# RWKV in a two-layer hybrid backbone: both directions' inverses on the diagonal of one 128x128 square

## The chip, the core and the metric

The kernel runs on one core of a Trainium2 chip. The metric is the device time of one execution in microseconds (us); the kernel before took 3027.57 us, the median of three runs (3020.59 to 3033.45). Engines: TensorE (PE; PEld is its weight load), VectorE (DVE), ScalarE (ACT), GpSimd (POOL), and SyncE (SP), which issues the transfers.

## What is computed

Two layers of a backbone over 256 latent and 256 context tokens of 1024 features. A layer is a half-step SwiGLU, a token mixing of three branches (retention, windowed attention, RWKV-7) with gates and an output projection, and a second half-step SwiGLU. The change touches RWKV-7 alone: 8 heads of 64, a forward and a backward scan, first over the context, then over the latent tokens from the context's final state.

```python
def rwkv7_scan(r, w, k, a, v, kk, s0, reverse):
    def step(S, inp):
        r_t, w_t, k_t, a_t, v_t, kk_t = inp
        sa = -jnp.einsum('bhvk,bhk->bhv', S, kk_t)
        S = (S * w_t[:, :, None, :] + sa[..., None] * (kk_t * a_t)[:, :, None, :]
             + v_t[..., None] * k_t[:, :, None, :])
        return S, jnp.einsum('bhvk,bhk->bhv', S, r_t)
    ...
    ys_f, S_f = rwkv7_scan(r_s, *dirs_s[0], v_s, kk_s, zero_rw, False)
    ys_b, S_b = rwkv7_scan(r_s, *dirs_s[1], v_s, kk_s, zero_rw, True)
    yx_f, _ = rwkv7_scan(r_x, *dirs_x[0], v_x, kk_x, S_f, False)
    yx_b, _ = rwkv7_scan(r_x, *dirs_x[1], v_x, kk_x, S_b, True)
    rwkv_x = rwkv_output(yx_f + yx_b, r_x, v_x, dirs_x, g_x, p)
```

## The kernel before

The big weight products (`mm3`, L186 to L188) run in three passes of a split format (fp32r, a high and a low part); one such pass is one TensorE instruction. All other products are f32, and each is two instructions in the trace. Weights come by DMA as `raw`, ScalarE makes `whi` (L114), VectorE `wlo` (L115).

RWKV works on chunks of 64 tokens: 4 chunks a stream, 2 streams (0 context, 1 latent), 4 pairs of heads, 2 layers. That is 16 rounds; the context of layer 1 needs no outputs, so 12 of the 16 make outputs (`want_y`). A round has five parts:
- `rw_prep` makes decays, and for each direction the operands `ar` (alpha, rho) and `kb` (kappa, beta). L945 transposes `kb` to `kbT`. L961 makes the Gram products; VectorE masks them into `gk` (L966) and, for outputs, into `tg` rows 64 to 127 (L968). ScalarE cuts the 32x32 diagonal blocks out (L964), and GpSimd inverts them (L989, L990).
- `rw_merge` fetches the inverted blocks as `z`. ScalarE (L1007) and VectorE (L1008) put them on the diagonal of `tg` rows 0 to 63, products of 32x32 (L1016, L1021) make the blocks off the diagonal. There is one `tg` tile for each stream and direction: 64 rows for the inverse, 64 for the triangular part of the outputs.
- `rw_vals` centres the values, one product for each chunk on 64 of the rows (L1033), and ScalarE copies them into `ve` for each direction (L1035, L1036) and into a block-diagonal tile `vb` (L1039).
- `rw_chain` goes through the chunks, j = 0 to 3, forward from the first and backward from the last, one direction after the other, each in one PSUM tile of the two under `rx`. For one direction: L1058 and L1060 add up values and state; L1062 (ScalarE) negates; L1065 is the inverse times that, two products for the two heads on a 64x64 tile; L1067 (ScalarE) copies the result into `ve`; L1069 makes the state's update, L1081 (VectorE) blends it into the state; L1086 multiplies the triangular part, again two 64x64 products; L1088 to L1092 (VectorE) add up the outputs `ya` on rows 64 to 127.
- `rw_out` normalises the outputs and multiplies gate and bonus.

The order of the work in token mixing is written as a list of names (`ORDER`: A and C are `rw_prep` of the two streams, B and D the rest, with retention, attention and gates between). Within that, a scheduler at build time puts the instructions of each engine in a row by its own estimates; the engines then run their rows in order.

```python
for j in range(4):
    for d in range(2):
        q = j if d == 0 else 3 - j
        x = ps("rx")
        PE.matmul(x[0:n, 0:128], gk[d][:, q, 0:n], vb[:, q], ...)
```

## Time and profile before

| | |
|---|---|
| median of 3 runs | 3027.57 us |
| span of the profiled execution | 3030.5 us |
| TensorE busy | 2924.9 us, 97% |
| VectorE busy | 2042.5 us, 67% |
| ScalarE busy | 1322.2 us, 44% |
| GpSimd busy | 382.4 us, 13% |
| mean granted TensorE clock | 0.967 |

The profile is of one execution. Busy times of TensorE count an instruction from its start to its modelled end, and neighbours overlap. The clock is given in parts of 2.4 GHz; a granted 0.50 is 1.2 GHz. The token mixing of layer 0 lies between some 400 and 1350 us, that of layer 1 between 2100 and 2830 us.

### The profile page before, as it was taken

What the parts mean: (1) busy time and instruction counts of PE and PEld (TensorE: products, weight loads), DVE (VectorE), ACT (ScalarE), POOL (GpSimd) and SP (SyncE); (2) the same over time, 40 slices, a digit from 0 to 9 for tenths busy, and PEclk for the clock granted to TensorE, in tenths of its full rate; (3) what the DMA queues carried; (4) which work ended last, traced back from release to release, by engine and by line L of the source; (5) the groups of instructions that cost most, each with busy time, mean ns of one, the idle gap of its engine ahead of it and who ended that gap; (6) DMA issues with size and microseconds to landing.
All of it is one profiled execution on the core that took longest, in us unless ns stands there. A gap on an engine that the chain in (4) does not pass through costs nothing.

```text
span 3030.5 us, 49119 instructions
## 1 busy us (share of the span) xinstructions
PE 2924.9 (97%) x17249; PEld 2436.6 (80%) x17249; DVE 2042.5 (67%) x4625; ACT 1322.2 (44%) x2832; POOL 382.4 (13%) x1076
## 2 busy tenths in 40 slices
PE   8999998999989999999999999999999999989999
PEld 7888887777777777888888888888778788778999
DVE  7977678774684565666756566566777676657755
ACT  3222246554454544343223332233656465555554
POOL 0000003332032121000000000000043433230000
PEclk9999999897989999999999999999979898999999
DMA  7655445341343144544535344444544244156554
GB/s 271 232 182 190 151 127 159 103 127 31 110 131 92 50 138 141 178 136 160 190 134 169 95 157 161 132 135 139 164 123 128 74 143 120 38 175 191 175 185 157
DMA packets 276439, 431.48 MB, mean 142 GB/s; under 512 B 80608, under 2 KB 98144, under 8 KB 276192
## 3 DMA queue, kind: packets, MB, share of 16 engines
q1 hardware_dynamic: 276192, 428.35, 44.8%
q8 instruction: 135, 2.21, 0.3%
q14 instruction: 112, 0.92, 0.1%
HBM read 398.74 MB, written 25.82 MB: 140 GB/s over the span
## 4 chain that ended last, share of the span: by engine, by line
PE 84%; POOL 5%; DVE 4%; DMA 3%; issue 2%; ACT 1%; SPq 1%; POOLq 0%; DVEq 0%; ACTq 0%
PE ps_mm L187 21%; PE ps_mm L186 21%; PE ps_mm L188 21%; POOL cst L990 2%; POOL cst L989 2%; PE ps_rf L961 2%; PE ps_mm L364 1%; PE ps_sc L532 1%; PE ps_po L542 1%; PE ps_po L762 1%; PE ps_rx L1065 1%; PE ps_rx L1058 1%; PE ps_rx L1069 1%; DVE wlo L115 1%; PE ps_rx L1086 1%
## 5 line engine op out<-in xcount | busy, mean ns | idle before, releaser
L114 ACT CAST whi<-raw 128x512 fp32r<-128x512 f32 x1070 | 648.6, 618 | 921.6 <-PE ps_mm L187 729.5
L115 DVE TENSOR_TENSOR wlo<-raw,whi 128x512 fp32r<-128x512 f32 x1070 | 728.9, 691 | 379.1 <-PE ps_mm L188 231.6
L186 PE MATMUL ps_mm<-hall,whi 128*128 128x512 f32 (+1 forms) x2320 | 846.6, 365 | 5.3 <-DVE cst L203 3.3
L188 PE MATMUL ps_mm<-hall,wlo 128*128 128x512 f32 (+1 forms) x2320 | 845.4, 365 | 2.1 <-DVE wlo L115 2.1
L187 PE MATMUL ps_mm<-hall,whi 128*128 128x512 f32 (+1 forms) x2320 | 840.1, 362 | 0.4 <-DVE hall L214 0.4
L186 PEld LDWEIGHTS ps_mm<-hall,whi 128*128 128x128 f32 x2320 | 444.1, 192 | 81.5 <-issue 8.3
L188 PEld LDWEIGHTS ps_mm<-hall,wlo 128*128 128x128 f32 x2320 | 443.0, 191 | 78.4 <-issue 3.9
L187 PEld LDWEIGHTS ps_mm<-hall,whi 128*128 128x128 f32 x2320 | 443.7, 191 | 72.8 <-issue 0.9
L186 PE MATMUL ps_mm<-hid,whi 128*128 128x512 f32 (+1 forms) x737 | 260.6, 354 | 0.0
L187 PE MATMUL ps_mm<-hid,whi 128*128 128x512 f32 (+1 forms) x737 | 260.0, 354 | 0.0
L188 PE MATMUL ps_mm<-hid,wlo 128*128 128x512 f32 (+1 forms) x737 | 257.5, 354 | 0.0
L989 POOL TENSOR_TENSOR cst<-acc,cst 128x60 f32<-128x60 f32 (+24 forms) x496 | 172.6, 348 | 490.2 <-DMA acc<-ad__11118 54.1
L841 POOL TENSOR_TENSOR ll<-lora,lh 64x256 fp32r<-64x256 f32 x16 | 11.9, 744 | 1475.1 <-ACT lh L838 1062.7
L990 POOL TENSOR_TENSOR cst<-cst 128x60 f32<-128x60 f32 (+24 forms) x496 | 178.6, 360 | 38.3
L236 DVE SCALAR_TENSOR_TENSOR ft<-m,cd 128x1024 bf16<-128x1024 f32 x136 | 162.7, 1218 | 6.5 <-DMA m<-ada 6.5
L237 DVE SCALAR_TENSOR_TENSOR m<-m,cd 128x1024 f32<-128x1024 f32 x136 | 165.0, 1218 | 0.7
L186 PEld LDWEIGHTS ps_mm<-hid,whi 128*128 128x128 f32 x737 | 139.2, 189 | 19.5
L187 PEld LDWEIGHTS ps_mm<-hid,whi 128*128 128x128 f32 x737 | 139.1, 189 | 19.3
L188 PEld LDWEIGHTS ps_mm<-hid,wlo 128*128 128x128 f32 x737 | 138.5, 189 | 19.5
L187 PE MATMUL ps_mm<-wlo,hall 128*128 128x256 f32 x416 | 132.7, 319 | 15.2 <-DVE wlo L115 14.9
L373 DVE SCALAR_TENSOR_TENSOR x<-ps_mm,cst,x 128x256 f32<-128x256 f32 x136 | 60.9, 480 | 103.6 <-PE ps_mm L188 101.3
L186 PE MATMUL ps_mm<-whi,hall 128*128 128x256 f32 x416 | 121.7, 294 | 0.2
(326 smaller groups left out, 4369.2 us busy)
## 6 DMA issues: line engine op xcount, KB each, us to landing
m<-ada SPq DMA_DIRECT2D x136, 512.0 KB, 4.3
raw<-w1b SPq DMA_DIRECT2D x271, 256.0 KB, 3.2
raw<-w0b SPq DMA_DIRECT2D x270, 256.0 KB, 2.9
raw<-w0a SPq DMA_DIRECT2D x132, 256.0 KB, 2.9
raw<-w0c SPq DMA_DIRECT2D x132, 256.0 KB, 3.0
raw<-w1a SPq DMA_DIRECT2D x132, 256.0 KB, 2.9
raw<-w1c SPq DMA_DIRECT2D x132, 256.0 KB, 3.0
gd<-ft SPq DMA_DIRECT2D x24, 256.0 KB, 2.6
```

Of the source, the lines that this page charges most:

```text
L114: nc.scalar.copy(hi, raw)
L115: nc.vector.tensor_sub(lo, raw, hi.bitcast(F32))
L186: PE.matmul(o, w[0], h[0], start=start, stop=False)
L187: PE.matmul(o, w[0], h[1], start=False, stop=False)
L188: PE.matmul(o, w[1], h[0], start=False, stop=stop)
L236: V.scalar_tensor_tensor(junk, raw, 1.0, st["cond"][0], ALU.mult, ALU.mult, accum_out=md[:, kt, 0:1])
L237: V.scalar_tensor_tensor(raw, raw, 1.0, st["cond"][1], ALU.mult, ALU.mult, accum_out=md[:, kt, 1:2])
L364: PE.matmul(o[:, p], w[k, j][q], hl(H[k], p)[0], start=(k == 0 and q == 0 and p.start == c.start), stop=False)
L373: V.scalar_tensor_tensor(xs[n][:, CS[s]], o[:, CS[s]], gate[:, n, s:s + 1], xs[n][:, CS[s]], ALU.mult, ALU.add)
L961: PE.matmul(ov[:, q, 0:n], kb[d][hs, q].rearrange("p a t -> p (a t)"), ar[d][hs, q].rearrange("p a t -> p (a t)")[:, 0:n], start=True, sto ...
L989: G.tensor_tensor(w, acc[j // 16][:, j % 16, j + 1:32].unsqueeze(1).to_broadcast([128, m, n]), tt[:, 0:m, j:j + 1].to_broadcast([128, m, n ...
L990: G.tensor_tensor(tt[:, 0:m, j + 1:32], tt[:, 0:m, j + 1:32], w, ALU.add)
```

## The change

The two directions share tiles. `tg` is gone; for each stream there are `tt` and `tr`, each 128x128 for a head and a step: the forward inverse on the rows and columns 0 to 63, the backward one on 64 to 127, in `tr` the triangular parts likewise; the two other quarters hold zeros, set once a layer by GpSimd (L1156) in place of small loads of zeros. The backward direction's chunks lie in reversed order, so that step j of both directions is one slot. To fit, the backward direction keeps alpha and rho, kappa and beta, and its values on the other half of the rows.

`rw_chain` takes both directions in one step: two PSUM tiles, `xa` and `xb`; the values and states of both directions, both negations, then one product a head for both inverses (L1076, a 128x128 tile, 64 columns), two copies, both state updates, and one product a head for both triangular parts (L1101). The outputs gather on both halves of the rows: two ScalarE copies and two VectorE sums a step, and `rw_out` adds the halves. `rw_vals` centres two chunks by one product (L1043), with copies of half the size. In `rw_merge` the copies of the inverse follow the products, and the backward blocks go through a tile of their own.

```diff
     def rw_merge(X, st):
-        z, tn, xm = mk([64, 2, 8, 32], "z", 2), mk([32, 16, 32], "rb", 3)[:, 0:8], mk([64, 16, 32], "rb", 3)[:, 0:8]
+        z, tb, xm = mk([64, 2, 8, 32], "z", 2), mk([64, 16, 32], "rb", 3), mk([64, 16, 32], "rb", 3)[:, 0:8]
+        tn, zt = tb[0:32, 0:8], tb[:, 8:16]
...
-        tg = X["tg"]
-        tu = [tg[d].rearrange("p h c t -> p (h c) t") for d in range(2)]
+        hc = lambda t: t.rearrange("p (h c) t -> p h c t", h=2)
+        fw, bw = X["tt"][0:64, :, :, 0:64], X["tt"][64:128, :, ::-1, 64:128]
         V.transpose(fl(tn), fl(z[0:32, 0]))
         for b in range(2):
             bs = slice(32 * b, 32 * b + 32)
-            A.copy(tu[0][bs, :, bs], z[bs, 0])
-            V.transpose(tu[1][bs, :, bs], z[bs, 1])
+            V.transpose(fl(zt[bs]), fl(z[bs, 1]))
...
+        for b in range(2):
+            bs = slice(32 * b, 32 * b + 32)
+            A.copy(fw[bs, :, :, bs], hc(z[bs, 0]))
+            A.copy(bw[bs, :, :, bs], hc(zt[bs]))
...
     def rw_vals(s, R, st, want_y, X):
-        for q in range(4):
-            PE.matmul(o[0:64, q * 128:q * 128 + 128], v[:, c.start + q * 64:c.start + q * 64 + 64], st["cm"], start=True, stop=True)
-        ov = o.rearrange("p (c d) -> p c d", c=4)
-        A.copy(ve[0][0:64], ov[0:64])
-        A.copy(ve[1][0:64], ov[0:64])
-        for h in range(2):
-            hs = slice(64 * h, 64 * h + 64)
-            A.copy(vb[hs, :, hs], ov[0:64, :, hs])
+        for i in range(2):
+            PE.matmul(o[:, i * 128:i * 128 + 128], v[:, c.start + i * 128:c.start + i * 128 + 128], st["cm"], start=True, stop=True)
+        ov = o[:, 0:256].rearrange("p (c d) -> p c d", c=2)
+        for i in range(2):
+            A.copy(ve[0][64:128, i::2], ov[HV[i]])
+            A.copy(ve[1][0:64, i::2], ov[HV[i]])
+            for h in range(2):
+                A.copy(vb[HV[h], i::2, HV[h]], ov[HV[i], :, HV[h]])
...
     def rw_chain(l, p, s, R, st, want_y, want_u, X):
         for j in range(4):
+            qs = (j, 3 - j)
+            xa, xb = ps("rx"), ps("rx")
+            for d, q in enumerate(qs):
+                U = R["U"][d]
+                rows = slice(0, 128) if want_y else HV[d]
+                xd = xa[rows, d * 128:d * 128 + 128]
+                PE.matmul(xd, gk[d][:, q, rows], vb[:, q], start=True, stop=(U is None))
+                if U is not None:
+                    PE.matmul(xd, ar[d][:, q].rearrange("p a t -> p (a t)")[:, rows], U, start=False, stop=True)
+            rr = sm(128, "rr", 2)
             for d in range(2):
-                A.activation(rr, x[0:64, 0:128], AF.Copy, scale=-1.0)
-                for h in range(2):
-                    hs = slice(64 * h, 64 * h + 64)
-                    PE.matmul(x[64:128, 128 + 64 * h:192 + 64 * h], tg[d][0:64, h, q], rr[:, hs],
-                              start=True, stop=True)
-                A.copy(ve[d][64:128, q], x[64:128, 128:256])
+                A.activation(rr[HV[d]], xa[HV[d], d * 128:d * 128 + 128], AF.Copy, scale=-1.0)
+            for h in range(2):
+                PE.matmul(xa[:, 256 + 64 * h:320 + 64 * h], tt[:, h, j], rr[:, HV[h]], start=True, stop=True)
+            for d, q in enumerate(qs):
+                A.copy(ve[d][HV[d], q], xa[HV[d], 256:384])
...
-                if want_y:
-                    for h in range(2):
-                        hs = slice(64 * h, 64 * h + 64)
-                        PE.matmul(x[64:128, 384 + 64 * h:448 + 64 * h], tg[d][64:128, h, q], ve[d][64:128, q, hs], start=True, stop=True)
-                    if q in seen:
-                        V.tensor_tensor(ya[64:128, q], ya[64:128, q], x[64:128, 0:128], ALU.add)
-                        V.tensor_tensor(ya[64:128, q], ya[64:128, q], x[64:128, 384:512], ALU.add)
-                    else:
-                        V.tensor_copy(ya[64:128, q], x[64:128, 0:128])
-                        V.tensor_tensor(ya[64:128, q], ya[64:128, q], x[64:128, 384:512], ALU.add)
-                        seen.add(q)
+            if want_y:
+                uu = sm(128, "uu", 2)
+                V.tensor_copy(uu, xa[:, 256:384])
+                for d, q in enumerate(qs):
+                    A.copy(ya[HV[1 - d], q], xa[HV[1 - d], d * 128:d * 128 + 128])
+                for h in range(2):
+                    PE.matmul(xb[:, 256 + 64 * h:320 + 64 * h], tr[:, h, j], uu[:, HV[h]], start=True, stop=True)
+                for d, q in enumerate(qs):
+                    V.tensor_tensor(ya[HV[1 - d], q], ya[HV[1 - d], q], xb[HV[1 - d], 256:384], ALU.add)
...
     def mix_consts(l, mark):
-        st["tg"] = {(s, d): mk([128, 2, 4, 64], "tg", 4) for s in range(2) for d in range(2)}
+        st["tt"], st["tr"] = ([mk([128, 2, 4, 128], n, 2) for _ in range(2)] for n in ("tt", "tr"))
+        for t in (*st["tt"], *st["tr"]):
+            G.memset(t, 0.0)
```

Three places show how the rows of instructions change. A row with xN holds N products in a run; names behind a line are output, inputs and the size of the output.

TensorE in layer 0, heads' pair 0, latent tokens, third step of the chain; L762, L759, L742, L743 and L746 are attention's products. Before:

```order
L762 MATMUL ps_po<-aT,kv 64x128 x4
L759 MATMUL ps_ap<-cst,ae 128x128 x3
L1065 MATMUL ps_rx<-cst,tg 64x64 x2
L759 MATMUL ps_ap<-cst,ae 128x128
L742 MATMUL ps_sc<-kd,qT 128x512
L743 MATMUL ps_sc<-kl,qT 128x512
L746 MATMUL ps_sc<-pa,cst 128x128
L188 MATMUL ps_mm<-hall,wlo 128x512
L1065 MATMUL ps_rx<-cst,tg 64x64 x2
L186 MATMUL ps_mm<-hall,whi 128x512
```

And now:

```order
L187 MATMUL ps_mm<-hall,whi 128x512
L188 MATMUL ps_mm<-hall,wlo 128x512
L762 MATMUL ps_po<-aT,kv 64x128 x4
L1076 MATMUL ps_rx<-cst,tt 128x64 x2
L186 MATMUL ps_mm<-hall,whi 128x512
```

Where two groups of two 64x64 products stood apart, one for each direction, one group of two stands for both.

TensorE in layer 0, pair 0, context tokens: the end of `rw_merge` and the centred values. Before:

```order
L542 MATMUL ps_po<-ft 128x128 x2
L1016 MATMUL ps_rx<-rb,cst 32x32 x8
L1016 MATMUL ps_rx<-z,cst 32x32 x8
L1033 MATMUL ps_rx<-cst,rr_v 64x128 x4
L542 MATMUL ps_po<-ft 128x128 x2
```

And now:

```order
L542 MATMUL ps_po<-ft 128x128 x2
L1022 MATMUL ps_rx<-rb,cst 32x32 x8
L1022 MATMUL ps_rx<-z,cst 32x32 x8
L1043 MATMUL ps_rx<-cst,rr_v 128x128 x2
L542 MATMUL ps_po<-ft 128x128 x2
```

Four products on half of the columns of the array become two on all of them, in the same place.

ScalarE in the same chain as the first place; L548, L560 and L572 belong to retention and gates. Before:

```order
L1062 ACTIVATE cst<-ps_rx 64x128
L1067 COPY ve<-ps_rx 64x128
L1062 ACTIVATE cst<-ps_rx 64x128
L548 ACTIVATE ft,cst<-ps_po 128x128 x2
L1074 ACTIVATE cst<-cst 128x128
```

And now:

```order
L1074 ACTIVATE cst<-ps_rx 64x128 x2
L548 ACTIVATE ft,cst<-ps_po 128x128 x4
L560 ACTIVATE ft<-ps_mm 128x512
L572 ACTIVATE ft<-ps_mm 128x512
L1078 COPY ve<-ps_rx 64x128 x2
L1099 COPY rb<-ps_rx 64x128 x2
```

The negations (L1062, now L1074) and the value copies (L1067, now L1078) of the two directions stand in pairs, and the output copies (L1099) follow.

## Rows read from the trace of the kernel before

**Rows 1.** The page: span, busy time by engine, the chain by engine.

```profile
span 3030.5 us, 49119 instructions
PE 2924.9 (97%) x17249; PEld 2436.6 (80%) x17249; DVE 2042.5 (67%) x4625; ACT 1322.2 (44%) x2832; POOL 382.4 (13%) x1076
PE 84%; POOL 5%; DVE 4%; DMA 3%; issue 2%; ACT 1%; SPq 1%; POOLq 0%; DVEq 0%; ACTq 0%
```

**Rows 2.** Span of the core and its mean granted clock.

```profile
core 0: 3030.5 us, clock 0.967
```

**Rows 3.** One window: PE, PEld, DVE, ACT, POOL busy; clock, DMA share, GB/s.

```profile
696.00:727.00 31.00, 30.90 (x160) 22.20 (x161) 11.46 (x32) 10.62 (x31) 7.79 (x28) 0.50 0.11 29
```

**Rows 4.** TensorE groups by shape: busy us, mean ns, idle before.

```profile
L1065 PE MATMUL ps_rx<-cst,tg 64*64 64x64 f32 x512 | 55.1, 234 | 1.9 <-ACT cst L1062 1.8
...
L1086 PE MATMUL ps_rx<-ve,tg 64*64 64x64 f32 x384 | 39.9, 232 | 4.7 <-DVE cst L1081 3.7 <-ACT ve L1067 0.9
...
L1033 PE MATMUL ps_rx<-cst,rr_v 128*64 128x128 f32 x128 | 19.7, 303 | 1.3 <-DVE ft L539 1.3
```

**Rows 5.** TensorE timeline: start us, us, line, tile of the array, form; one quad.

```profile
2283.26 0.28 PE L186 MATMUL ps_mm<-hall,whi 128*128 128x256 f32 x1
2283.48 0.44 PE L1065 MATMUL ps_rx<-cst,tg 64*64 64x64 f32 x4
...
2284.07 0.28 PE L188 MATMUL ps_mm<-hall,wlo 128*128 128x256 f32 x1
2284.19 0.28 PE L186 MATMUL ps_mm<-hall,whi 128*128 128x256 f32 x1
```

**Rows 6.** TensorE timeline: two quads in a row.

```profile
2543.12 0.28 PE L186 MATMUL ps_mm<-whi,hall 128*128 128x256 f32 x1
2543.33 0.68 PE L1065 MATMUL ps_rx<-cst,tg 64*64 64x64 f32 x8
...
2544.15 0.28 PE L188 MATMUL ps_mm<-whi,hall 128*128 128x256 f32 x1
```

**Rows 7.** TensorE timeline: four f32 instructions on the full tile.

```profile
823.09 0.28 PE L186 MATMUL ps_mm<-whi,hall 128*128 128x256 f32 x1
823.21 0.61 PE L1069 MATMUL ps_rx<-ve,kbT 128*128 128x128 f32 x4
...
823.77 0.28 PE L188 MATMUL ps_mm<-whi,hall 128*128 128x256 f32 x1
```

**Rows 8.** TensorE timeline: eight on a 64x128 tile, 64 columns moving.

```profile
2181.49 0.28 PE L186 MATMUL ps_mm<-whi,hall 128*128 128x256 f32 x1
2181.70 1.10 PE L961 MATMUL ps_rf<-ar,kb 64*128 64x64 f32 x8
...
2182.95 0.28 PE L188 MATMUL ps_mm<-whi,hall 128*128 128x256 f32 x1
```

**Rows 9.** ScalarE and VectorE groups by shape: busy us, mean ns, idle before.

```profile
L1062 ACT ACTIVATE cst<-ps_rx 64x128 f32<-64x128 f32 x128 | 33.6, 269 | 48.2 <-PE ps_rx L1060 39.5 <-PE ps_rx L1058 7.4
L1067 ACT COPY ve<-ps_rx 64x128 f32<-64x128 f32 x128 | 32.3, 260 | 48.1 <-PE ps_rx L1065 41.8 <-PE ps_rx L1086 4.5
...
L1035 ACT COPY ve<-ps_rx 64x512 f32<-64x512 f32 x16 | 9.2, 578 | 8.2 <-PE ps_rx L1033 7.9
...
L790 DVE MEMSET cst<- 128x1024 f32 x1 | 0.9, 912 | 1.0 <-PEq L1335 1.0
```

**Rows 10.** TensorE's waits: for whom, us in total, times, longest.

```profile
PE ps_rx L1069 <- ACT ve L1067: 9.4, 6, 6.4
...
PE ps_rx L1058 <- DVE rb L1092: 4.4, 4, 1.7
PE ps_rx L1086 <- DVE cst L1081: 3.7, 7, 1.1
...
PE ps_rx L1058 <- DVE rb L1089: 2.7, 3, 1.0
```

More of the change, by code (lines that the diff above doesn't have):

```diff
@@ L792, in rw_consts @@
         return dict(bones=const("bones", 128), cm=const("cm", 128), mg=const("mg", 256).rearrange("p (d x) -> p d x", d=2),
[L793 removed]
+                    one=const("ones", 64), ks=const("ks", 2), ub=[[ub[:, d, b] for b in range(2)] for d in range(2)],
                     vbd=per[:, 800:1312].rearrange("p (q x) -> p q x", q=4))
@@ L1098, in rw_out @@
         vec = st["vec"]
+        sqt = mk([128, 512], "rb", 3)
+        back = sqt[64:128].rearrange("p (c x) -> p c x", c=4)
+        A.copy(back, ya[0:64])
+        V.tensor_tensor(ya[64:128], ya[64:128], back, ALU.add)
         y = ya[64:128].rearrange("p c (h d) -> p (c h) d", d=64)
-        sqt = mk([128, 512], "rb", 3)
         sq = sqt[64:128].rearrange("p (u d) -> p u d", d=64)
@@ L1145, in mix_consts @@
             att_consts(st)
-            for s in range(2):
-                for b in range(2):
-                    z = st["tg"][s, b][32 - 32 * b:64 - 32 * b].rearrange("p h c t -> p (h c) t")
-                    SP.dma_start(out=z[:, :, 32 * b:32 * b + 32], in_=I["zero"])
         return st
@@ L1261, in shape_consts @@
         incl = before | np.eye(64, dtype=bool)
-        mg[0:64, d, 0:64] = before
-        mg[0:64, d, 64:] = incl
-        mg[64:, d, 64:] = incl * f(0.5)
+        own, other = halves[d], halves[1 - d]
+        mg[other, d, own] = before
+        mg[other, d, other] = incl
+        mg[own, d, other] = incl * f(0.5)
+        ks[own, d] = 0.5
     c["mg"] = mg
```

70 lines of the change are left out of this document (33 added, 37 removed).

## The prediction

> **What bounds the kernel now.** I read the page first: over a span of 3030.5 us TensorE is busy 97%, VectorE 67%, ScalarE 44%, and 84% of the chain that ended last is TensorE's own work, one instruction after another [rows 1]. So an instruction taken off TensorE pays in full, and one added on VectorE, ScalarE or GpSimd pays only where TensorE comes to wait for it. Second, the groups by shape: what the change touches on TensorE is L1065 (inverse times values, 512 instructions, 55.1 us), L1086 (the triangular part for the outputs, 384, 39.9 us) and L1033 (centred values, 128, 19.7 us) [rows 4]. Every f32 product is two instructions, so these are 256, 192 and 64 products. Third, the clock: the mean grant is 0.967 [rows 2], so some 200 us (0.033 / 0.5 of the span) ran at 1.2 instead of 2.4 GHz. One such stretch is 696 to 727 us, where TensorE was busy 30.9 of 31 us and granted 0.50 [rows 3].
>
> Busy times hold the tail of each instruction, which the next one overlaps, so I do not subtract them. I price an instruction by how much later the wide products behind it start. Wide 256-column products follow each other every 0.12 us (2284.07 to 2284.19) [rows 5].
> - One quad of 64x64 tiles (two products): from the wide product ahead (2283.26) to the second one behind (2284.07) is 0.81 us; less two steps of 0.12, it costs 0.57 [rows 5].
> - Eight 64x64 instructions in a row: 2543.12 to 2544.15, so 1.03 - 0.24 = 0.79 [rows 6]. The four more cost 0.22, or 0.055 each; 0.57 - 0.22 = 0.35 us is left as a fixed price of a narrow group among wide ones, 0.175 a side.
> - Four f32 instructions with a full 128x128 tile (L1069): 823.09 to 823.77, so 0.68 - 0.24 = 0.44: 0.11 each and no fixed price [rows 7].
> - Eight with a 64x128 tile and only 64 moving columns: 2181.49 to 2182.95, so 1.46 - 0.24 = 1.22; less 0.35 that is 0.11 each [rows 8]. So half the moving columns against 128 stationary ones gain nothing.
>
> The products of the new L1076 and L1101 (full tile, 64 columns) are of no form that ran before. They lie between 0.055 an instruction (L1065, same columns [rows 6]) and 0.11 (same stationary width [rows 7, 8]); I take 0.11.
>
> **TensorE, part by part.** I counted groups and neighbours in the two orders.
> - L1065 becomes L1076. Before: 256 products in 110 groups (21 of four, 83 of two, 6 of one): 256 x 0.11 + 110 x 0.35 = 66.7; on 61 of the 220 sides the neighbour is narrow too, 61 x 0.175 = 10.7 off: 56.0 us. After: 128 products of 0.22 = 28.2, and 29 sides on which a narrow neighbour now meets a full tile, 5.1: 33.3. Gain 22.7.
> - L1086 becomes L1101. Before: 192 x 0.11 + 75 x 0.35 - 32 x 0.175 = 41.8. After: 96 x 0.22 + 8 x 0.175 = 22.5. Gain 19.3.
> - L1033 becomes L1043, half as many products of the same 128 columns, with 128 stationary columns for 64. Before: 64 x 0.22 + 16 x 0.35 - 21 x 0.175 = 16.0. After: 32 x 0.22 + 19 x 0.175 = 10.3. Gain 5.7.
> - The 32x32 products of the merge, transposes, Gram products and state products keep number and size.
> Sum: 47.7 us at the full clock; 47.7 / 0.967 = 49 with the share at the low one.
>
> A rule speaks against this. What the rows show: an f32 instruction rises from 0.055 to 0.11 us when its tile goes from 64 to 128 stationary columns [rows 6, 8]. The Trainium skill, "TensorE: Matmul & The Clock Gate", section "LDWEIGHTS (loading the stationary operand)", says that a weight load takes time by its columns, whatever its rows; the trace agrees. By that rule alone half the products at twice the load gain nothing at L1065 and L1086, and only L1033's 7 us would be left. The rows add the 0.35 us of a narrow group; the skill's "TensorEngine Tiling (Array Packing)", section "Key Properties", says that changing the tiling mode drains the engine, and the trace agrees with 0.35 us for the way in and out.
>
> **The other engines.** ScalarE gets 204 more instructions: two output copies a step (96, at L1067's 0.26 us), four more value copies a merge, two more copies of the inverse a merge, one copy an output [rows 9]; some 60 us on an engine busy 44%. Hidden, as long as they do not stand ahead of something TensorE waits for. One place does: the copies of values now number eight of half the size for four, about 1 us more of ScalarE ahead of a chain's first blend (sixteen chains: 0 to 16 us; L1035 takes 0.58 us for the whole width [rows 9]). I take 3, as attention, retention or weight products stand behind most of them in the order. VectorE loses 36 instructions: no price. GpSimd gets eight memsets (VectorE's takes 0.91 us for one of that size [rows 9]) where it has nothing else to do; if that cover were gone, some 8 us. The eight zero loads leave SyncE's queue: nothing waited for them.
>
> **The chain's waits.** TensorE now waits 4.4 + 2.7 us at L1058 for an accumulation tile that the sums of outputs (L1092, L1089) still read, 9.4 at L1069 for ScalarE's value copy and 3.7 at L1086 [rows 10]. The first goes: in the new step the first tile is read by copies only, and they do not wait for the output product. What is late next there is the blended state (four blends a step on VectorE). Against that, a step now holds both directions: two negations, then two copies, must all be done before one product, 0.27 us more for each pair [rows 9]. Before, one direction's products could fill the other's wait. In the order, stretches with under 1 us of other work between a product and the one that needs it are 40 of 352 before and 35 of 288 after, so I take -3 for this, within -7 and +20.
>
> Total: -49 + 3 - 3 = -49. On the profiled execution's own 3030.5 us that is 2981; the median of the runs is 2.9 us under that execution, so 2978. I put 2980.
>
> **Rivals.**
> 1. *The fixed price isn't saved* (weight columns alone count, for instance because the scheduler puts the new groups beside narrow ones). For it: the doubling shows [rows 6, 8]. Against: both forms stand among the same wide products [rows 5, 7], 0.57 against 0.44 for four instructions, and the new group does the work of two quads. What is left is L1033's 32 products of 0.22, 7 us: 3021. Chance 0.12. The skill's section on LDWEIGHTS is this rival's rule.
> 2. *Lock-step starves TensorE (slower).* Each of the 64 steps has three turns (ScalarE, ScalarE, VectorE) in which neither direction has a product ready; an uncovered one costs about 1 us (4.4 us in 4 waits at L1058, 9.4 in 6 at L1069 [rows 10]). From 49 more uncovered turns of 192 the gain is gone, from 64 on it is slower by over 0.5%; at 70: 3028 - 49 + 70 = 3049. For it: L1069's longest wait is 6.4 us. Against: the order's 35 short stretches, no more than before. Chance 0.10.
> 3. *The clock turns.* The new order moves every stretch of small f32 products, and in such a stretch the clock fell [rows 3]. If 60 us more run at 1.2 GHz, 30 us are given back: 3008. If 60 us less do, 2948. Chance 0.12 for the bad side; the good side is in the range.
> 4. *It doesn't do what it says.* The order shows 128 and 96 products where 256 and 192 stood; no chance worth a number.
>
> **How the numbers follow.** Forecast 2980, chance 0.66, its own range 2950 to 3010 (all quads alone or all in pairs, -7 to +20 of waits). What a measurement of this kernel can tell from no change is about 0.5%, 15 us. Faster by more: the forecast's 0.66 and half of rival 3, 0.72. Within: rival 1, the rest of rival 3 and a little of rival 2, 0.20. Slower: 0.08. The range 2952 to 3022 leaves out rival 2 and the ends of the clock.
>
> **What would show it.** After: L1076 with 256 instructions and L1101 with 192, four of them costing 0.44 between wide products (0.22 would make me wrong on the columns, 0.57 or more on the fixed price); TensorE's busy time down by 40 to 60 us; waits at the chain's lines near 20 us together; the mean clock within 0.96 to 0.975. Wrong if the busy time falls and the idle time rises by as much (rival 2), or if the clock's mean is under 0.955 (rival 3).

## The result, and the profile of the changed kernel

The changed kernel takes 3053.32 us (median of five runs, 3045.29 to 3059.82) against 3027.57 for the kernel before (five runs, 3020.59 to 3038.62): a ratio of 1.0074, 95% interval 1.0053 to 1.0094. It is 0.7% slower where 1.6% faster was forecast, outside the range. Ratios below are to the kernel before in the same session, whose median lay between 3026.6 and 3031.6. Two executions that ran far longer than the rest of their kernel (7445 us, the outputs on one half, and 3207 us, the other list in the changed kernel) are left out of the ratios.

The page of the changed kernel (span, busy time by engine, the chain that ended last), and then the core's span and mean granted clock; compare [rows 1, 2]:

```profile
span 3043.5 us, 47906 instructions
...
PE 2882.9 (95%) x16737; PEld 2419.7 (80%) x16737; DVE 2015.8 (66%) x4589; ACT 1346.0 (44%) x3036; POOL 396.3 (13%) x1084
...
PE 81%; DVE 8%; POOL 3%; DMA 3%; ACT 2%; issue 2%; SPq 0%; DVEq 0%; POOLq 0%; ACTq 0%
```

```profile
core 0: 3043.5 us, clock 0.958
```

TensorE's busy time fell by 42.0 us, as forecast. Its idle time, span less busy, rose from 105.6 to 160.6, by 55.0. The difference is the 13.0 us that the profiled span grew. VectorE's share of the chain that ended last went from 4% to 8%.

TensorE's groups by shape (tile of the array, form, count, busy us, mean ns, idle before) for the three changed lines; compare [rows 4]:

```profile
L1076 PE MATMUL ps_rx<-cst,tt 128*128 128x64 f32 x256 | 40.5, 282 | 14.3 <-ACT cst L1074 14.3
...
L1101 PE MATMUL ps_rx<-cst,tr 128*128 128x64 f32 x192 | 29.9, 281 | 4.9 <-DVE cst L1093 2.8 <-DVE cst L1097 1.9
...
L1043 PE MATMUL ps_rx<-cst,rr_v 128*128 128x128 f32 x64 | 12.6, 326 | 1.8 <-DVE ft L539 1.8
```

Counts are as forecast. So is the price: in TensorE's timeline (start us, duration) four of the new instructions between wide products take 2264.70 - 2264.02 - 2 x 0.12 = 0.44 us; the median of the 11 such places with no wait in them is 0.45.

```profile
2264.02 0.28 PE L187 MATMUL ps_mm<-wlo,hall 128*128 128x256 f32 x1
2264.14 0.55 PE L1076 MATMUL ps_rx<-cst,tt 128*128 128x64 f32 x4
2264.50 0.37 PE L188 MATMUL ps_mm<-whi,hall 128*128 128x256 f32 x1
2264.70 0.28 PE L186 MATMUL ps_mm<-whi,hall 128*128 128x256 f32 x1
```

Much of the idle time lies at the end of layer 0's token mixing. Windows (us; PE, PEld, DVE, ACT, POOL busy; granted clock, DMA share, GB/s) of the kernel before, first, and of the changed kernel:

```profile
1260.00:1280.00 20.00, 20.00 (x94) 15.71 (x93) 13.54 (x32) 6.07 (x10) 0.00 (x0) 1.00 0.33 101
1280.00:1300.00 20.00, 20.00 (x90) 16.56 (x89) 16.00 (x28) 10.69 (x16) 0.00 (x0) 1.00 0.85 296
2780.00:2800.00 20.00, 20.00 (x169) 20.00 (x168) 17.02 (x37) 9.94 (x19) 0.00 (x0) 1.00 0.85 274
2800.00:2820.00 20.00, 20.00 (x169) 20.00 (x168) 17.78 (x39) 12.32 (x25) 0.00 (x0) 1.00 0.75 221
```

```profile
1260.00:1280.00 20.00, 9.51 (x40) 7.92 (x40) 7.06 (x27) 8.27 (x19) 0.95 (x1) 0.57 0.21 68
1280.00:1300.00 20.00, 17.04 (x62) 13.31 (x63) 13.90 (x24) 7.04 (x13) 0.00 (x0) 0.74 0.57 170
2780.00:2800.00 20.00, 15.47 (x129) 15.00 (x127) 11.97 (x30) 8.61 (x22) 0.00 (x0) 0.97 0.71 243
2800.00:2820.00 20.00, 14.75 (x93) 13.94 (x94) 15.30 (x43) 7.98 (x17) 0.00 (x0) 0.68 0.05 10
696.00:727.00 31.00, 28.00 (x143) 21.59 (x141) 19.18 (x52) 16.40 (x44) 0.38 (x2) 0.84 0.16 52
```

TensorE was full there before; in the changed kernel it worked less than half of 20 us, and from 1263 on, while it waited between short products, the clock was down at 1.2 GHz for 27.3 us. The same happens near 2800, at the end of layer 1. (The stretch of [rows 3] got better: 0.84 for 0.50.) Over the whole span 256 us were granted 1.2 GHz where 201 were before.

TensorE's waits (for whom: total us, times, longest) name the place; compare [rows 10], which do not show `rw_out`'s transpose before (L1113, 2.1 us):

```profile
PE ps_mm L187 <- DVE wlo L115: 24.6, 29, 3.1
PE ps_rx L1126 <- DVE rb L1123: 15.4, 5, 6.1
PE ps_rx L1076 <- ACT cst L1074: 14.3, 11, 3.5
```

L1126 is that transpose now, 20.1 us in all with another wait of 4.7. TensorE's timeline in layer 0 from the last round's last chain product on, and VectorE's beside it (idle before an instruction and its releaser in brackets):

```profile
1273.43 1.11 PE L1101 MATMUL ps_rx<-cst,tr 128*128 128x64 f32 x4 [0.94 <-DVE cst L1097]
1280.67 0.66 PE L1126 MATMUL ps_rx<-cst,rb 64*128 64x64 f32 x4 [6.12 <-DVE rb L1123]
1281.26 1.22 PE L1127 MATMUL ps_rx<-lo,cst 128*128 128x256 f32 x2
1284.77 1.22 PE L186 MATMUL ps_mm<-ro,whi 128*128 128x512 f32 x2 [2.29 <-ACT ro L210]
```

```profile
1274.65 0.60 DVE L1103 TENSOR_TENSOR rb<-rb,ps_rx 64x128 f32<-64x128 f32 x2 [1.28 <-PE ps_rx L1101]
1275.94 0.69 DVE L1112 TENSOR_TENSOR rb<-rb 64x512 f32<-64x512 f32 x1 [0.68 <-ACT rb L1111]
1277.32 0.68 DVE L1118 TENSOR_REDUCE cst<-rb 64x8 f32<-64x512 f32 x1 [0.69 <-ACT rb L1115]
...
1279.84 0.69 DVE L1123 TENSOR_TENSOR rb<-rb,cst 64x512 f32<-64x512 f32 x1
```

From 1273 to 1285 TensorE stands behind one chain of short operations, most of them on VectorE. The branch products that need this output have nothing left ahead of them; the first of them starts at 1284.77.

**The reading that this rests on.** The rounds of RWKV follow one another in one string: in the changed kernel a round's merge starts 0.2 to 2.3 us behind the output of the round before, or behind the chain where there is no output; in the kernel before mostly 1 to 5 us behind, twice later (7.4 and 21.7). From the starts in the timeline I take five figures for each kernel: the string of layer 0 (start of the first merge product to start of the last output's transposes), the way from there to layer 1's first merge, the string of layer 1, the rest to the end, and TensorE's idle time.

| kernel | string, layer 0 | to layer 1 | string, layer 1 | to the end | idle |
|---|---|---|---|---|---|
| before | 738.2 | 963.7 | 536.8 | 254.3 | 105.6 |
| changed | 740.8 | 964.1 | 558.4 | 240.3 | 160.6 |
| before, longer string | 800.5 | 961.9 | 610.7 | 238.7 | 178.3 |
| changed, rounds first | 720.1 | 973.6 | 549.5 | 239.8 | 148.2 |
| before, other list | 720.2 | 984.1 | 507.4 | 270.0 | 116.2 |
| changed, outputs on one half, rounds first | 713.3 | 977.9 | 547.4 | 239.8 | 140.8 |

The rows below the second are experiments of the next section. The second and fourth column have a floor, 961 to 964 and 239 to 240 us: where they stand on it, the last output ends the stage; where they stand above it, TensorE still had wide products to do and its sum ends the stage. Before, layer 0 stood on the floor and layer 1 some 14 us above. So TensorE's sum and the string ended together, and a saving on TensorE could win at most those 14 us in layer 1 unless the strings got shorter too. They got longer, by 2.6 and 21.6 us: 2.4 (start of the first merge) + 2.6 + 0.4 + 21.6 - 14.0 = 13.0 us. That the five figures add up to the difference of the spans is so by their making; the reading is which of them moved.

The strings fall into parts (starts on TensorE, summed over a layer's eight rounds):

| kernel, layer | merges and the wait before them | values to the chain's first product | chain, first to last product | last product to the output's transposes |
|---|---|---|---|---|
| before, 0 | 73.3 | 78.8 | 458.5 | 127.7 |
| changed, 0 | 58.5 | 51.8 | 491.3 | 139.2 |
| before, 1 | 59.7 | 54.3 | 361.4 | 61.4 |
| changed, 1 | 40.9 | 48.4 | 402.4 | 66.7 |

So it is the chain walked in step that got longer, by 32.8 and 41.0 us, and the output by 11.5 and 5.3; what merges, values and the waits between rounds became shorter was used up by it.

### The profile page after: what moved, and what is told of

It is laid out like the page before. It is cut to its first block, busy times and chain, and to the rows that moved or that the text cites. A ratio compares the mean times of both kernels' runs of the same rounds, so it can differ in the third digit from the quotient of the medians.

```text
span 3043.5 us, 47906 instructions
## 1 busy us (share of the span) xinstructions
PE 2882.9 (95%) x16737; PEld 2419.7 (80%) x16737; DVE 2015.8 (66%) x4589; ACT 1346.0 (44%) x3036; POOL 396.3 (13%) x1084
## 4 chain that ended last, share of the span: by engine, by line
PE 81%; DVE 8%; POOL 3%; DMA 3%; ACT 2%; issue 2%; SPq 0%; DVEq 0%; POOLq 0%; ACTq 0%
PE ps_mm L186 20%; PE ps_mm L187 20%; PE ps_mm L188 20%; DVE wlo L115 2%; POOL cst L995 2%; PE ps_rf L964 2%; POOL cst L994 1%; PE ps_mm L364 1%; PE ps_sc L532 1%; PE ps_po L542 1%; PE ps_po L762 1%; PE ps_rx L364 1%; PE ps_rx L1076 1%; PE ps_rx L1069 1%; DMA z<-td 1%
## 5 line engine op out<-in xcount | busy, mean ns | idle before, releaser
L187 PE MATMUL ps_mm<-hall,whi 128*128 128x512 f32 (+1 forms) x2320 | 840.6, 362 | 0.0
L114 ACT CAST whi<-raw 128x512 fp32r<-128x512 f32 x1070 | 626.6, 617 | 427.3 <-PE ps_mm L187 275.7
L115 DVE TENSOR_TENSOR wlo<-raw,whi 128x512 fp32r<-128x512 f32 x1070 | 719.5, 689 | 96.1 <-ACT whi L114 49.2
L187 PEld LDWEIGHTS ps_mm<-hall,whi 128*128 128x128 f32 x2320 | 442.7, 191 | 71.8 <-issue 1.0
L187 PE MATMUL ps_mm<-hid,whi 128*128 128x512 f32 (+1 forms) x737 | 260.0, 354 | 0.0
L401 DVE TENSOR_TENSOR ft<-ft,ps_mm 128x512 f32<-128x512 f32 (+1 forms) x80 | 49.6, 620 | 215.8 <-PE ps_mm L188 182.8
L995 POOL TENSOR_TENSOR cst<-cst 128x60 f32<-128x60 f32 (+24 forms) x496 | 185.1, 373 | 38.1
L187 PE MATMUL ps_mm<-wlo,hall 128*128 128x256 f32 x416 | 133.1, 320 | 25.1 <-DVE wlo L115 24.6
L187 PEld LDWEIGHTS ps_mm<-hid,whi 128*128 128x128 f32 x737 | 139.0, 189 | 19.4
```

What stands on the lines that cost most here:

```text
L114: nc.scalar.copy(hi, raw)
L115: nc.vector.tensor_sub(lo, raw, hi.bitcast(F32))
L187: PE.matmul(o, w[0], h[1], start=False, stop=False)
L995: G.tensor_tensor(tt[:, 0:m, j + 1:32], tt[:, 0:m, j + 1:32], w, ALU.add)
```

## The experiments

Theory A: TensorE's saving is real, and is lost because the last round's output ends each stage. Theory B, the forecast's rival 2: working in step starves TensorE all through the rounds. Theory C: the clock alone sets the loss.

**Nothing waits for the last output**, in both kernels:

```diff
-            if p < 3:
-                SP.dma_start(out=st["od"][p, :, CS[s]], in_=R["r"][:, CS[s]])
-            else:
-                st["last"] = R["r"]
+            SP.dma_start(out=st["od"][p, :, CS[s]], in_=R["r"][:, CS[s]])
...
-        split(hl(rw[3], c), st["last"][:, c])
+        spilled(st, 2, 1, S, rw[3:], mid)
```

> The changed kernel, but nothing waits for the last round of RWKV in a layer (pair 3, latent tokens): its output is stored like the other pairs' and not read; the last branch reads pair 2's output a second time in its place, so the output of pair 3 is left out. The round itself is still computed, with every product. Theory A (the end of the stage): TensorE did save its some 42 us, and the whole of it is lost where the last round's serial string ends after the wide products have run out, at 1262 to 1290 us and at 2797 to 2820 us. Then this kernel is 30 to 45 us faster than the changed one, 3008 to 3023 us against 3053, a little below the kernel before, TensorE idles 90 to 110 us in all instead of 145, and neither place shows a half clock any more. Theory B (starving): working in step leaves TensorE waiting everywhere, so freeing the end brings under 10 us: 3043 to 3053. Theory C (clock alone): the half-clock time is 256 us as in the changed kernel and turns up elsewhere; 3035 to 3050.

> The same edit on the kernel before (the output of pair 3's latent tokens is computed and stored, not read; pair 2's is read twice). Theory A: before, the end of the last round was covered by wide products (TensorE without a gap from 1180 to 1300 us), so nothing is to be had: 3020 to 3030 us, under 8 us from 3027.6. If it gains as much as the changed kernel does by the same edit (30 us or more), theory A is wrong: then the end of the stage was just as bare before.

The changed kernel became 3016.84 us, 0.9944 of before (0.9921 to 0.9968); the kernel before stayed at 1.0007 (0.9993 to 1.0020). So the end of the stage costs the changed kernel 1.3%, some 37 us between the medians, and the kernel before nothing clear of noise. Theory C's range (3035 to 3050) is missed, and the time at 1.2 GHz, 229 us, didn't turn up elsewhere. The freed kernel's windows where the changed one stood bare:

```profile
1260.00:1280.00 20.00, 20.00 (x98) 16.75 (x97) 14.21 (x28) 11.08 (x21) 0.00 (x0) 1.00 0.73 268
1280.00:1300.00 20.00, 20.00 (x97) 16.56 (x96) 14.83 (x29) 7.92 (x18) 0.00 (x0) 1.00 0.63 193
```

Idle fell to 137.7 us, not to the 90 to 110 expected: 34 us more than in the freed kernel before (103.4). Little of that is theory B's. Counting waits of over 0.15 us, TensorE waits at the chain's own lines 18.6 us there, against 16.3 in the freed kernel before. The rest lies around the chain: `rw_out` 12.7 against 1.8, `rw_prep` 11.6 against 5.9, the heads of retention and attention 16.7 against 4.9, the weight products 32.0 against 24.6 (their largest group, L187's waits for VectorE's low parts, 22.6 against 16.2). What ties these to the change isn't shown.

**More work on TensorE that nothing waits for**, in both kernels:

```diff
             o = ps("mm")
+            for _ in range(4 * len(CS) // len(S)):
+                PE.matmul(o[:, c], W.get(W.pos)[0], hl(H[0], c)[0], start=True, stop=True)
             dense(W, f"g{g}", H, c, o)
```

> The changed kernel with more TensorE work that nothing waits for: each of the 48 gate products repeats its first pass (4 times with 512 columns in layer 0, 8 times with 256 in layer 1), some 0.22 us and 0.11 us each, 21 us a layer and 42 us in all, spread over the mixing stages. The repeated passes are overwritten. Theory A: the stage ends with the serial string of RWKV's rounds, and TensorE had work to spare: the time rises by less than half of the added 42 us, 3053 to 3075, and the bare gaps at the two ends shrink. Theory B, or any reading in which TensorE's sum of work sets the time: 3053 + 42 = 3095, at least 3088.

> The same 42 us of TensorE work added to the kernel before. If TensorE's sum set the time there, as the forecast took it: 3027.6 + 42 = 3070 (3060 to 3078). If the serial string of rounds already set it before, well below that: 3030 to 3050. Theory A expects the first of the two, since before no gap stood at the ends of the stages.

The kernel before took all of it: 3074.12 us, 1.0141 (1.0120 to 1.0162), 43 us for 42 added. The changed one went to 3081.62, 1.0169 (1.0144 to 1.0193), from 1.0074: 29 us. It had slack, but for a third of the work where I had said more than half. The strings show why: the added products stand in the same row as the rounds, and the strings grew by 19.3 and 9.8 us; in the kernel before by 22.8 and 31.0, down to the floor at both ends. So the two bounds aren't independent: work put among the rounds delays their string too, and in the kernel before this run can't tell one bound from the other.

**A longer string, the same TensorE work**, in the kernel before:

```diff
                 A.activation(rr, x[0:64, 0:128], AF.Copy, scale=-1.0)
+                for _ in range(4):
+                    A.activation(rr, rr, AF.Copy, scale=-1.0)
```

> The kernel before with a longer string: in each step of the chain the negated sum is negated four times more in place by ScalarE (64x128, 0.27 to 0.28 us each, so the result is the same), about 1.1 us a step of a direction, 4.4 us a round at least on the string and up to 8.8 where the directions don't cover each other: 35 to 70 us a layer of string if every round follows the one before it at once. TensorE's work is unchanged; ScalarE gets some 140 us more beside 1322 of 3030. Theory A (the stage ends with the serial string of rounds as soon as it ends later than the wide products): the kernel gets 15 to 60 us slower (3045 to 3090), with bare gaps at the ends of the stages (near 1280 to 1330 and 2780 to 2840 us) like those of the changed kernel. If TensorE's sum alone set the time: 3027 to 3035.

3148.31 us, 1.0400 (1.0385 to 1.0415): 121 us, twice what I expected at most. The strings grew by 62.3 and 73.9 us, the ends went to the floor, and gaps stand at the ends of both stages, in layer 1 near 2900 us for the 2780 to 2840 expected. Windows of this kernel:

```profile
1300.00:1320.00 20.00, 16.63 (x113) 13.44 (x107) 4.62 (x15) 9.63 (x33) 0.00 (x0) 0.50 0.01 1
1320.00:1340.00 20.00, 11.81 (x62) 9.25 (x60) 7.82 (x29) 7.02 (x26) 0.00 (x0) 0.50 0.00 0
```

The string of rounds was a second bound of the kernel before, at hardly any distance from the first.

**The one product undone, the walk in step kept**: two 64x64 products for each direction in the place of L1076 and L1101.

```diff
-            for h in range(2):
-                PE.matmul(xa[:, 256 + 64 * h:320 + 64 * h], tt[:, h, j], rr[:, HV[h]], start=True, stop=True)
+            for w in HV:
+                for h in range(2):
+                    PE.matmul(xa[w, 256 + 64 * h:320 + 64 * h], tt[w, h, j, w], rr[w, HV[h]], start=True, stop=True)
...
```

> The changed kernel with the one product for both directions undone and the walk in step kept: L1076 and L1101 become two products for each direction, on the 64x64 quarters of the same tiles. TensorE's busy time goes back up by the forecast's 40 us or so, to 2915 to 2930, with two quads (1.14 us) in the place of one four (0.44) in each step. Theory A: the 0.7 us lies on the string in the inverse product, 2.8 us a round, so the ends of the stages come later by some 20 us a layer at most, and TensorE has less to spare: 3070 to 3095, 17 to 42 us above the changed kernel. Then the product for both does pay, and walking in step without it costs 45 to 65 us against before. Theory B (starving by the lock step, whatever the products take): the time stays at 3050 to 3062, since TensorE waits anyway.

3061.04 us, 1.0113 (1.0099 to 1.0128): only 0.4% above the changed kernel, and TensorE busy 2899.0, not 2915 to 2930. My price was wrong, as TensorE's timeline of this kernel shows:

```profile
2461.78 0.28 PE L186 MATMUL ps_mm<-whi,hall 128*128 128x256 f32 x1
2461.99 0.45 PE L1077 MATMUL ps_rx<-cst,tt 64*64 64x64 f32 x8
2462.38 0.39 PE L187 MATMUL ps_mm<-wlo,hall 128*128 128x256 f32 x1
2462.61 0.28 PE L188 MATMUL ps_mm<-whi,hall 128*128 128x256 f32 x1
```

Eight instructions cost 2462.61 - 2461.78 - 0.24 = 0.59 us (median of the 12 such places with no wait in them 0.58), where eight on one quarter of the array cost 0.79 [rows 6]. The two directions lie on opposite quarters here (in `tt` on the diagonal; in `tr` on the two quarters off it, not on the diagonal as the section on the change has it), and their instructions start in twos, 0.013 us apart. The Trainium skill, "TensorEngine Tiling (Array Packing)", section "Key Properties", says that different tiles can load and multiply in parallel; the trace agrees, with 0.58 against 0.79. So of the 0.69 us between two groups of four (2 x 0.57 [rows 5]) and one four on the full tile (0.45), 0.35 come from one group in place of two [rows 6], 0.21 from the opposite quarters, and 0.13 from the one product. For 64 + 48 groups that last part is 15 us, an estimate: busy time rose by 16.1, but with busy time at 1.2 GHz counted by half there is no rise (2775 us against the changed kernel's 2781). The time falls into theory B's range and below theory A's, but A's number came from the wrong price; between the two theories this run decides nothing.

**Another order alone**, in both kernels: merge, values, chain and output are placed ahead of anything else that is ready.

```diff
-                rw_back(l, int(j), "BD".index(k), S, st)
+                with tc.high_priority():
+                    rw_back(l, int(j), "BD".index(k), S, st)
```

> The changed kernel with another order alone: the scheduler is told to place the rounds' second half (merge, values, chain, output) ahead of anything else that is ready, where it went by the order of the program. Nothing is computed differently. In the row of TensorE the last output product of layer 0 stands some 17 us of wide products earlier than in the changed kernel, that of layer 1 in the same place. Theory A: the bare end of layer 0 (24.5 us lost there, 27.3 us at half clock) shrinks by 10 to 20 us, that of layer 1 by 0 to 5: 3030 to 3043. Theory B: no change, 3045 to 3060.

> The kernel before with the other order alone (the rounds' second half first). It gave the changed kernel 28 us back. Theory A: before, the string and the wide products ended together (a gap-free TensorE from 1180 to 1300 us), so an earlier string has nothing to win: 3018 to 3032. If it wins 15 us or more here too, the order's gain isn't what the change lost.

The changed kernel went to 3025.51, 0.9990 (0.9979 to 1.0000), 25 us back by the ratios (28 between the medians) with not one instruction different. Its strings are 20.7 and 8.9 us shorter, and layer 0 came 10 us off the floor. Layer 0's chains are back at 459.4 us, layer 1's at 392.6: in layer 0 the chain had been longer by its place in the rows and not by what it holds. The kernel before got slower, 3057.12, 1.0082 (1.0050 to 1.0114), against my expectation. Its profiled execution lies at the low end of its runs, 3037.7 us, and shows layer 0's string 14 us shorter, 984.4 us behind it and idle time unchanged (107.3): an earlier string won nothing, as theory A has it. The loss of this one execution is the clock's: 218 us at 1.2 GHz in the place of 201 is 8 us. The four slower executions were granted a mean of 0.955 to 0.958, this one 0.964; 0.006 to 0.009 of 3040 us is 18 to 27 us, an estimate, and they took 17 to 27 us longer than its 3039.51. Why this order is granted less isn't shown. With this order in both, the changed kernel is the faster one, by 0.9%: which of the two wins depends on the order.

**Two of the four ScalarE copies of a step on VectorE**:

```diff
-            for d in range(2):
-                A.activation(rr[HV[d]], xa[HV[d], d * 128:d * 128 + 128], AF.Copy, scale=-1.0)
+            A.activation(rr[HV[0]], xa[HV[0], 0:128], AF.Copy, scale=-1.0)
+            V.tensor_scalar(rr[HV[1]], xa[HV[1], 128:256], -1.0, None, ALU.mult)
...
-            for d, q in enumerate(qs):
-                A.copy(ve[d][HV[d], q], xa[HV[d], 256:384])
+            A.copy(ve[0][HV[0], qs[0]], xa[HV[0], 256:384])
+            V.tensor_copy(ve[1][HV[1], qs[1]], xa[HV[1], 256:384])
```

> The changed kernel with two of the four ScalarE copies of a step, the backward direction's negation and its value copy, made by VectorE beside ScalarE's forward ones. In step, the two of a kind stand one behind the other on ScalarE (0.28 us each); beside each other they take 0.29, so the string is 0.5 us a step shorter, 2 us a round, 16 us a layer. Theory A: the last output comes up to 16 us earlier in each layer and 5 to 30 us come back: 3023 to 3048. If the copies wait for their turn on a crowded VectorE (67% busy; at 1187 to 1206 us an output's fourteen short operations stood between full ones of 0.69 us), nothing comes back or it gets slower: 3050 to 3065.

3072.99 us, 1.0144 (1.0127 to 1.0162): worse by 20 us, more than either side expected. The strings grew by 18.7 and 8.3 us. The median time from one step's inverse product to the next is 14.3 us (13.8 in the changed kernel, 11.8 for one direction before), while the instructions of a step take under 4 us (four of ScalarE and four of VectorE of 0.28 each, three groups of products of 0.44). So most of a step is waiting for turns; that VectorE's row makes one wait longer than ScalarE's would explain this run, but isn't shown.

**The output's PSUM tile in another bank**, with the rounds first, so that a merge need not stand behind the output before it:

```diff
     def rw_out(l, p, s, R, st, ya, X):
...
-        o = ps("rx")
+        o = ps("sc")
```

> The changed kernel with the string of rounds unhooked: the output's PSUM tile (rw_out) comes from the bank of the scores (sc) and not from the two banks that chain, values and merge use (rx), so that a round's merge need not stand behind the output of the round before, as it did in every trace so far, some 1 us behind it; and the rounds go first, as in the run with the other order alone. In TensorE's row the merges now stand ahead of the outputs, and the last output of layer 0 stands 24 us of wide products earlier than with the order alone, that of layer 1 some 20. Theory A: with the string out of the way TensorE's sum is the bound, and its saving shows: 2985 to 3012, 15 to 42 us under the kernel before; the last products under the branch no longer wait bare. Theory B: 3020 to 3035, no better than the order alone. If the score bank makes attention and the outputs wait for each other, 3030 or more.

> The kernel before with the same two edits (the output's tile in the scores' bank, the rounds first). Theory A: before, TensorE's sum was met as well as the string, so unhooking the string gives little: 3010 to 3028. The distance between this kernel and the changed one with the same edits is then the change's own worth where only TensorE's sum counts: 20 to 42 us. If this one gains as much as the changed one, the change's saving isn't what the unhooking sets free, and theory A is wrong.

> As the changed kernel unhooked, but with the output's tile in the bank of attention's transposes (ap) in the place of the scores': another neighbour to collide with, the same unhooking. The last output stands where it stood with the scores' bank in layer 0 and 8 us later in layer 1. Theory A: within 10 us of the run with the scores' bank, 2985 to 3018. If the two differ by more than 15 us, the neighbour in the bank counts for more than the string.

3159.74 (1.0423, 1.0398 to 1.0448), 3152.86 (1.0401, 1.0372 to 1.0431), and 3049.53 with `ap` (1.0061, 1.0035 to 1.0086). The string was unhooked: four rounds of layer 0 were through at 803 us where the changed kernel was at 913. But then the next merge came only at 945; that outputs and attention's scores now take turns in one bank would explain it, but isn't shown. And where the rounds ran close together, no wide product stood among them (none of 229 and 378 instructions of TensorE in the two windows below, 113 of 319 and 196 of 546 in the changed kernel), TensorE waited between them, and the clock stayed at 1.2 GHz. Windows of the kernel with `sc`:

```profile
560.00:625.00 65.00, 48.45 (x230) 39.54 (x230) 34.06 (x107) 29.38 (x86) 29.84 (x86) 0.50 0.08 19
2345.00:2445.00 100.00, 76.55 (x380) 59.44 (x378) 38.73 (x116) 41.26 (x124) 42.09 (x131) 0.50 0.12 27
```

The changed kernel was granted 0.82 and 0.83 in these stretches. In all, 451 us ran at 1.2 GHz. Theory A's forecasts for all three runs (2985 to 3012, 3010 to 3028, 2985 to 3018) are missed, and the 20 to 42 us by which the changed kernel was to be ahead of the kernel before with these edits came out as 0.2% behind. With `ap` the kernel is 24 us slower than with the rounds first and nothing else. Since the two kernels with `sc` failed alike, by far more than the change is worth, the runs neither bear theory A out nor refute it; the 15 us that `sc` and `ap` were not to differ by became 110.

**The outputs gathered on one half of the rows.** What was still open was why the strings didn't get shorter. One candidate besides the chain is the output. This kernel takes out what the change added to `rw_out`, once alone and once with the rounds first:

```diff
-                    A.copy(ya[HV[1 - d], q], xa[HV[1 - d], d * 128:d * 128 + 128])
+                    src = xa[HV[1 - d], d * 128:d * 128 + 128]
+                    if j < 2:
+                        A.copy(ya[64:128, q], src)
+                    else:
+                        V.tensor_tensor(ya[64:128, q], ya[64:128, q], src, ALU.add)
...
-                    V.tensor_tensor(ya[HV[1 - d], q], ya[HV[1 - d], q], xb[HV[1 - d], 256:384], ALU.add)
+                    V.tensor_tensor(ya[64:128, q], ya[64:128, q], xb[HV[1 - d], 256:384], ALU.add)
...
-        A.copy(back, ya[0:64])
-        V.tensor_tensor(ya[64:128], ya[64:128], back, ALU.add)
```

> The changed kernel with the outputs of both directions gathered on the same half of the rows, as before: the backward direction's parts are added from PSUM into rows 64 to 127, so rw_out needs neither the ScalarE copy of 64x512 (0.62 us) nor the VectorE sum (0.69 us) ahead of the normalising; two short VectorE additions (0.29 us) take the place of two ScalarE copies in the last two steps. If the copy across is part of why the rounds' string is long, each round with outputs is 1.5 to 4 us shorter, 8 rounds in layer 0 and 4 in layer 1, and since the string ends the stages (theory A), 10 to 40 us come back: 3013 to 3043. If the string is long for the chain's own waits, nothing does: 3046 to 3060.

> The same with the rounds' second half placed first, as in the run of the other order alone (3025.5). That run had some 11 us of cover left at the end of layer 0 and none in layer 1, so what counts is layer 1's four rounds with outputs: 6 to 16 us if the copy across is on the string, 3009 to 3020, which would beat both kernels; 3022 to 3030 if not.

Alone: 3035.31, 1.0014 (0.9997 to 1.0030), 18 us back. In the profiled execution layer 0's string stayed (741.1) and layer 1's fell from 558.4 to 549.1. The bare way from the last chain product to the last output's transposes fell by 1.4 us in each layer (from 6.5 to 5.1 and from 6.4 to 5.0), 3 us of the 18; where the rest was won isn't shown. With the rounds first: 3021.89, 0.9972 (0.9959 to 0.9986), the one version with nothing left out that is clearly ahead of both kernels, by 0.3% against before. Its windows at the two ends show that layer 0 is covered and layer 1 not quite:

```profile
1260.00:1280.00 20.00, 20.00 (x89) 16.32 (x88) 11.73 (x20) 9.25 (x14) 0.00 (x0) 1.00 0.47 174
...
2780.00:2800.00 20.00, 18.16 (x129) 18.16 (x130) 16.54 (x39) 10.34 (x22) 0.00 (x0) 0.83 0.58 176
```

**Another list of the work**, in both: the last pairs' chains are named earlier in the last part of `ORDER`.

```diff
...
-G7 G8 P3 H6 G9 C3 B3 H7 D3 G10 G11
+C3 G7 B3 G8 P3 H6 D3 G9 H7 G10 G11
...
...
-D2 G7 A3 C3 G8 P3 B3 G9 G10 H6 H7 D3 G11
+A3 D2 C3 G7 B3 G8 P3 D3 G9 G10 H6 H7 G11
```

> The changed kernel with another list at the end of each stage: the last two pairs' chains (D2, B3, D3) are named ahead of gates and heads that stood before them, and nothing else. In TensorE's row the last outputs stand in the same places as in the changed kernel (the order of the list decides only between what is ready). Theory A: no earlier string, no gain, 3040 to 3062. If mere placement is worth tens of us, it can come out anywhere from 3020 to 3080.

> The same list in the kernel before. Its row has the last output of layer 0 some 22 us of wide products earlier, that of layer 1 some 14. Theory A: TensorE's sum is met there anyway, so nothing is won: 3018 to 3035. A loss of 20 us or more, as with the rounds first (3057), would mean that placement alone moves the kernel before by more than the change did.

1.0088 (1.0071 to 1.0105) and 1.0008 (0.9993 to 1.0023): both as theory A expects; no string is read of the changed kernel here. The kernel before is the telling one: its strings are 18 and 29 us shorter in the profile, its ends 20 and 16 us further above the floor, and its time is the same. There TensorE's sum was met whatever the string did.

## Why the prediction was wrong

TensorE's timeline of the kernel before, from the last output's transposes to the first branch product (it reads `ro`), in layer 0 and in layer 1:

```profile
1275.71 0.46 PE L1113 MATMUL ps_rx<-cst,rb 64*128 64x64 f32 x4
...
1278.74 0.40 PE L186 MATMUL ps_mm<-ro,whi 128*128 128x512 f32 x1
...
2776.18 0.46 PE L1113 MATMUL ps_rx<-cst,rb 64*128 64x64 f32 x4
...
2794.86 0.28 PE L186 MATMUL ps_mm<-ro,whi 128*128 128x256 f32 x1
```

- **TensorE's saving: right.** The price of four was 0.45 for the 0.44 forecast, busy time fell by 42.0 of the forecast 40 to 60. Counting busy time within the stretches at 1.2 GHz by half, TensorE's work is 2832 us before and 2781 after, 51 less against the sum of 47.7. The eight variants of the changed kernel without added work on TensorE that can be read lie at 2774 to 2779, those of the kernel before at 2814 to 2834, so it is the change's own. The reason was right in its larger part, one narrow group in place of two (0.35 us); that two directions on opposite quarters would by themselves have saved another 0.21, and the full tile but 0.13, was not seen.
- **"An instruction taken off TensorE pays in full": the step that failed.** A busy share of 97% and a chain that is 84% TensorE said only that TensorE had been the later of two bounds, not by how much. The other bound is the string of rounds, which the forecast had nowhere. The trace of before held the answer (the lines above). In layer 0 the first branch product reading `ro` starts 3.0 us behind the last output's transposes, in layer 1 18.7 us; bare, the same way takes 4.1 (1284.77 - 1280.67 in the changed kernel). So the wide work behind the string's end left nothing over in layer 0 and 14.6 us in layer 1. The runs show the tie: the end freed gives the changed kernel 37 us and the kernel before nothing, a longer string costs the kernel before 121 us with the same work on TensorE, and a shorter one alone wins it nothing.
- **"The chain's waits", -3 within -7 to +20: in its range, but not what counts.** All the waits of over 0.15 us at the chain's lines are 26.7 us (L1076 14.3) against 22.9 before, +3.8. I looked for TensorE's waits between the chain's products and judged cover by short stretches. That the chain itself takes 74 us longer, covered by other work until that runs out at the end of a stage, was in no term; nor was `rw_out`, where 20.1 us of waits appeared. In layer 0 another order alone takes the growth back; in layer 1 it takes back 10 of the 41 us, and what the rest is no run separates. One thing untested is VectorE's copy ahead of L1101 (L1097, 48 of 0.29 us), which the forecast did not list.
- **The copies of values, +3:** the way from the values to the chain's first product got shorter (by 27.0 and 5.9 us), so nothing speaks for this loss.
- **"One copy an output", ScalarE's, costed at nothing: wrong.** The condition that I named (not ahead of something TensorE waits for) is what it broke: the copy and VectorE's sum behind it stand ahead of the last output. Gathering the outputs on one half gave back 18 us, of which 3 can be seen at the two ends.
- **Rival 2 (3049, chance 0.10)** gave about the right time by luck. Its mark appeared (busy time down, idle time up by more), but its mechanism, TensorE's waits between the steps, is worth 3.8 us at the chain's lines. Freed of the end alone the kernel is 0.6% faster than before. Of the 51 us, some 34 go into idle time spread around the chain, whose cause stays open; the end of the stages takes the rest and 20 more.
- **Rival 3, the clock:** 0.958, between its two marks. Of the 55 us more at 1.2 GHz, 41 are the two bare ends (27.3 and 13.7): there the low clock goes with TensorE's waiting, and is gone in the kernel whose end is freed.

## What to carry to other kernels

A busy engine is the bound only as far as the cover behind it reaches: before costing a saving on it, find the serial string that ends the stage, and read how many us of other work stand between its last product and the first instruction that needs it. If that is nearly nothing, the two bounds are tied, and a cheaper busy engine has to come with a shorter string. An operation added to the string is then paid for, however idle its engine: the copy and the sum ahead of the last output took 1.4 us of each stage's bare end.

## What the runs showed of the hardware

- f32 products on opposite 64x64 quarters of the array run side by side: 0.58 us for eight against 0.79 on one quarter, the starts in twos 0.013 us apart.
- In 100 us of small f32 products without one wide product among them the clock was granted 0.50 throughout; in the same 100 us of the changed kernel, with 196 wide ones between, 0.83. The first of these kernels, with 451 us at 1.2 GHz, took 134 us more than the one with the rounds first and the outputs in their old bank, which had 236 us.
